# Stick-breaking attention trunk on one core: elementwise work moved from VectorE to GpSimd, and ten instead of nine of sixteen steps with seven products

## The chip, the cores and the metric

The kernel runs on one core of a Trainium2 chip. The core has TensorE (PE, with PEld for the loading of weights), VectorE (DVE), ScalarE (ACT), GpSimd (POOL) and SyncE (SP, which here only issues transfers). The metric is the device time of one execution in microseconds; less is better.

## The reference, cut to what matters

The input `x` has 256 rows of 4096 numbers. One layer of attention is computed and added to it, and a final norm follows (`DEPTH` is 1, so the convolution branch of the file is not reached):

```python
h = x + attn_branch(rms_norm(x, norm_attn), w_in_attn, w_out_attn)
return rms_norm(h, final_norm)

def attn_branch(xn, w_in, w_out):
    q, k, v, g = jnp.split(xn @ w_in, 4, axis=-1)      # 32 heads of 128
    o = stick_breaking_attention(q, k, v)
    return (o * jax.nn.silu(g)) @ w_out

# in the attention, for s < t (strictly causal):
log_fail = where(causal, log_sigmoid(-z), 0)           # z = q k^T / sqrt(128)
a = where(causal, exp(log_sigmoid(z) + suffix_sum(log_fail)), 0);  out = a @ v
```

All of it is float32. The two weight matrices are 4096 x 16384 and 4096 x 4096.

## The kernel before, in words

**Three matmuls for one product.** Every large product is made with float32 values that are split into a high part of type fp32r and a low part, the rest: `h = fp32r(f)`, `l = f - h`. `mm3` (line 780) adds `hh`, `hl` and `lh` in PSUM. ACT makes the high part of a weight block (`wh`, a copy that converts) and DVE the low part (`wl = raw - wh`, by `minus`, line 257). The same is done for the stationary side, the 128 x 128 blocks of x ("forms" `sh`, `sl`) or of the heads (`oh`, `ol`): `both_parts` (line 496).

**Units and steps.** The work of PE is cut into 21 units, each of 16 steps. Units 0 to 15 make the input projection: each has two column blocks of 256 of q and k, and two of gate and v. Then come three units of the output projection with two column blocks of 512 each, and two single ones. A step takes two of the 32 chunks of 128 along the summed dimension. The two row blocks, the two chunks and the two column blocks give a 2 x 2 times 2 x 2 product: a plain step makes eight products, a "mixed" one follows a scheme of Strassen and Winograd. Steps whose number is in `SEVEN` (line 42) need seven products; for them DVE makes sums of weight blocks (`sums`, line 424: three instructions of 128 x 512), and one of the sums comes from an accumulating transfer (`add_block`, line 401: two DMAs issued by POOL that add HBM data to the tile). Other mixed steps take eight products with fewer parts to split: two wide ones (128 x 1024) in place of three wide and one half one (`SEVEN_PARTS`, `EIGHT_PARTS`). Units 0 and 16 are plain, units 1 to 15, 17 and 18 mixed (17 of them), 19 and 20 single, with four products a step.

**Forms.** `blocks_of` (line 528) loads two chunks of x transposed, scales them by the norm's gains, splits them, and calls `sums_of` (line 502) for the sums of blocks that the mixed units need: one instruction of 128 x 256 for an eight-step, four of 128 x 128 for a seven-step, then `both_parts` for what came out. This happens in unit 0. `blocks_of_heads` (line 927) does the same for the output projection with the heads' results, which were spilled to HBM and are fetched again; `again` (line 950) makes one block anew for the single units.

**Heads.** A unit of the input projection yields two heads. `combine` (line 676) adds up the PSUM banks, `gate` (line 763) makes SiLU of the gate, and `head` (line 795) runs one head as a chain: transposes, scores `z`, softplus in four ACT instructions, DVE `f = max(z, 0) + f`, the causal mask of `f` (DVE, minimum with `bound`, a tile of 3e38 and zeros that is made once, line 595), split into `fh` and `fl`, the scan as four matmuls with a triangle of minus ones, two ACT instructions for the weights `a`, the mask of `a` (DVE), and the product with v.

**The end.** `block_out` (line 1007) adds x, sums the squares and multiplies by the gains of the final norm (`h * grow`, DVE); `finish` (line 1107) scales and stores.

**What sets the order.** The program is written out by a planner, `Plan`. Each piece of work is a generator that asks for engine time with a cost and a key; a small event simulation gives each engine the waiting item with the smallest key, and the instructions are issued in that order. `dve`, `act`, `ten` and `moved` (lines 338 to 354) state costs; `until` waits for a name, `take` and `give` are rings of buffers (seven `raw` tiles, five wide and two half pairs of `wh`/`wl`). On the chip each engine runs its own list strictly in that order, with semaphores where data is needed; the planner's times no longer matter there. POOL's list before holds the accumulating DMAs, the spills and fetches of heads, and a few set-up instructions.

In the profile nearly all instructions carry line 115, the line of the planner's helper, so groups are told apart by their tiles.

## Time and profile before

| | |
|---|---|
| median of 3 runs | 1757.85 us (1756.26 to 1759.46) |
| profiled execution, its span from first to last instruction | 1754.0 us |
| what lies around the span (median less span; no other time of the profiled execution is given) | 3.85 us |
| mean granted TensorE clock | 0.997 |
| DMA | 405.86 MB, mean 231 GB/s |

How to read the profile: busy time is the union of an engine's instructions. A group's row gives engine, operation, tiles (written<-read, buffer numbers left out), shapes, count, then busy time and mean ns of one, then the idle time of the engine just before these instructions and what ended it. In the list of waits, "A <- B: total, times, longest" is the time that A's instructions waited for B's. The chain that ended last goes back from the last instruction to what released it, step by step. A row of the timeline is start, duration, engine, instruction. DVE instructions overlap a little when they follow each other, so a group's busy time can be less than count times mean.

### The profile page before, as it was taken

Reading aid. Unit: us, or ns where it says so; the run is one execution under the profiler, and the core shown is the slowest. Engines: PE = TensorE matmul, PEld = TensorE weight load, DVE = VectorE, ACT = ScalarE, POOL = GpSimd, SP = SyncE. Lnnn points to the kernel's source line nnn. Section 1 sums busy time; section 2 is a strip of 40 time slices with the busy share of each in tenths; the row PEclk is TensorE's granted clock in tenths of the full one; section 3 lists DMA queues with packets and bytes.
Section 4 is the critical chain, followed back from the end, with each engine's and each line's share of the span. In section 5 each row is a group of like instructions: output and inputs, shape, how many; then the busy total and the mean of one; then the engine's idle time right before and its main releaser. Section 6 shows DMA issues by size and latency. Waiting matters only on the chain.

```text
span 1754.0 us, 24699 instructions
## 1 busy us (share of the span) xinstructions
PE 1736.9 (99%) x7806; PEld 1427.1 (81%) x7806; DVE 1560.4 (89%) x1971; ACT 1166.4 (67%) x1594; POOL 295.7 (17%) x364
## 2 busy tenths in 40 slices
PE   8999999999999999999999999999999999999997
PEld 6888888888888888888888888888888888888885
DVE  7889999999999999999999999999999997899963
ACT  7975767676767676767676767676767675666543
POOL 0012121111111121211111111111112111111100
PEclk9999999999999999999999999999999999999998
DMA  9968777777777878787878787878786877889874
GB/s 340 316 192 224 230 218 229 223 223 226 222 228 217 239 210 239 208 245 210 240 208 245 208 239 206 242 202 245 200 246 200 262 244 239 229 245 271 257 236 156
DMA packets 242867, 405.86 MB, mean 231 GB/s; under 512 B 27520, under 2 KB 67968, under 8 KB 242736
## 3 DMA queue, kind: packets, MB, share of 16 engines
q1 hardware_dynamic: 193968, 352.15, 60.8%
q0 software_dynamic: 47184, 49.76, 17.3%
q10 hardware_dynamic: 1584, 2.38, 0.4%
q8 instruction: 61, 1.00, 0.2%
q14 instruction: 70, 0.57, 0.1%
HBM read 396.05 MB, written 8.13 MB: 230 GB/s over the span
## 4 chain that ended last, share of the span: by engine, by line
PE 92%; DVE 3%; issue 2%; DMA 2%; ACT 1%; SPq 0%; ACTq 0%; DVEq 0%
PE acc L115 87%; PE z L115 2%; DVE wl L115 2%; PE o L115 2%; DMA raw<-in_w_in_dram 1%; PE tr L115 1%; ACT wh L115 1%; DVE raw L115 0%; ACT h L115 0%; SPq L115 0%; DMA xres<-in_x_dram 0%; DMA raw<-in_w_out_dram 0%; ACTq L115 0%; DVE gv_sb L115 0%; DVE h L115 0%
## 5 line engine op out<-in xcount | busy, mean ns | idle before, releaser
L115 ACT CAST wh<-raw 128x1024 fp32r<-128x1024 f32 (+1 forms) x948 | 886.1, 976 | 476.1 <-issue 173.3
L115 DVE TENSOR_TENSOR wl<-raw,wh 128x1024 fp32r<-128x1024 f32 (+1 forms) x948 | 1032.1, 1131 | 125.3 <-ACT wh L115 118.6
L115 PE MATMUL acc<-wh,sh 128*128 128x512 f32 x1913 | 762.6, 399 | 2.4 <-DVE sh L115 2.1
L115 PE MATMUL acc<-wh,sl 128*128 128x512 f32 x1913 | 746.2, 390 | 0.0
L115 PE MATMUL acc<-wl,sh 128*128 128x512 f32 x1913 | 744.9, 389 | 0.8 <-DVE wl L115 0.8
L115 PEld LDWEIGHTS acc<-wh,sh 128*128 128x128 f32 x1913 | 359.4, 188 | 77.3 <-DVE gv_sb L115 3.9
L115 PEld LDWEIGHTS acc<-wh,sl 128*128 128x128 f32 x1913 | 359.1, 188 | 76.9 <-DVE sl L115 0.8
L115 PEld LDWEIGHTS acc<-wl,sh 128*128 128x128 f32 x1913 | 359.7, 188 | 71.5 <-DVE wl L115 1.5
L115 POOL DMA_DIRECT2D raw<-in_w_in_dram x270 | 236.1, 987 | 1075.7 <-DMA raw<-in_w_in_dram 403.1
L115 DVE TENSOR_TENSOR raw<-raw,raw 128x512 f32<-128x512 f32 x306 | 210.3, 687 | 5.1
L115 PE MATMUL acc<-wh,oh 128*128 128x512 f32 x494 | 193.2, 391 | 0.0
L115 PE MATMUL acc<-wl,oh 128*128 128x512 f32 x494 | 192.4, 389 | 0.6 <-DVE wl L115 0.6
L115 PE MATMUL acc<-wh,ol 128*128 128x512 f32 x494 | 192.3, 389 | 0.0
L115 PEld LDWEIGHTS acc<-wl,oh 128*128 128x128 f32 x494 | 92.8, 188 | 20.5 <-DVE wl L115 1.2
L115 PEld LDWEIGHTS acc<-wh,oh 128*128 128x128 f32 x494 | 92.8, 188 | 19.3 <-DVE gv_sb L115 0.4
L115 PEld LDWEIGHTS acc<-wh,ol 128*128 128x128 f32 x494 | 92.7, 188 | 19.2
L115 DVE TENSOR_TENSOR raw<-raw 128x512 f32<-128x512 f32 x153 | 104.5, 683 | 0.0
L115 POOL DMA_DIRECT2D raw<-in_w_out_dram x36 | 31.6, 992 | 132.5 <-DMA raw<-in_w_out_dram 66.2
L115 ACT ACTIVATE f<-f 128x384 f32<-128x384 f32 x96 | 50.5, 526 | 3.0
L115 DVE SCALAR_TENSOR_TENSOR f<-z,f 128x384 f32<-128x384 f32 x32 | 17.8, 557 | 31.2 <-ACT f L115 31.2
L115 POOL DMA_DIRECT2D p<-spill x33 | 20.3, 696 | 129.6 <-DVE ol L115 94.0
L115 ACT ACTIVATE gl<-gl 128x512 f32<-128x512 f32 x48 | 30.0, 625 | 7.3 <-DVE gl L115 7.3
(90 smaller groups left out, 745.9 us busy)
## 6 DMA issues: line engine op xcount, KB each, us to landing
raw<-in_w_in_dram SPq DMA_DIRECT2D x1020, 256.0 KB, 4.6
raw<-in_w_out_dram SPq DMA_DIRECT2D x256, 256.0 KB, 3.9
raw<-in_w_in_dram POOLq DMA_DIRECT2D x270, 128.0 KB, 5.2
raw<-in_w_out_dram POOLq DMA_DIRECT2D x36, 128.0 KB, 5.6
xr<-in_x_dram SPq DMA_DIRECT2D x16, 256.0 KB, 5.2
xres<-in_x_dram SPq DMA_DIRECT2D x16, 256.0 KB, 5.6
xs<-in_xT_dram SPq DMA_DIRECT2D x15, 256.0 KB, 5.3
spill<-gated POOLq DMA_DIRECT2D x15, 256.0 KB, 3.9
```

What stands on the lines that cost most here:

```text
L115: return self.tc.keep_in_program_order(getattr(self.engine, name)(*args, **kw))
```

## The change

Three things are done at once. `SEVEN` has ten steps and other ones. A cost function for POOL is added to the planner, and these pieces go from DVE to POOL: the subtraction that makes low parts of forms and of `f`, the sums of row blocks and of heads' blocks, the last product of the gate, and the final norm's gains; the two causal masks become an `affine_select` on POOL, and `bound` goes. Some keys are 1 to 3 us earlier. The low parts of weights (`wl`), the sums of weight blocks and all that reads PSUM stay on DVE. Here is the diff:

```diff
--- before.py
+++ after.py
@@ -39,7 +39,7 @@
 
 
 
-SEVEN = (1,3,5,7,8,10,11,13,14)
+SEVEN = (1, 2, 4, 5, 7, 8, 10, 11, 13, 14)
 RAW_BUFS = 7
 PAIRS = 5
 SINGLES = 2
@@ -87,6 +87,10 @@
 
 def scalar_ns(n):
     return 98 + n / 1.2
+
+
+def pool_ns(n):
+    return 200 + 2.2 * n
 
 
 def tensor_ns(n):
@@ -254,8 +258,8 @@
 
     tc.nc.scalar.preload_act_table_set("natural_log_exp_and_others")
 
-    def minus(out_, full, part):
-        nc.vector.tensor_tensor(out=out_, in0=full, in1=part.bitcast(F32), op=ALU.subtract)
+    def minus(out_, full, part, engine=None):
+        (engine or nc.vector).tensor_tensor(out=out_, in0=full, in1=part.bitcast(F32), op=ALU.subtract)
 
 
     units = []
@@ -345,6 +349,11 @@
         cost = sum(scalar_ns(m) for m in n) + 100 * (len(n) - 1)
         return nc.work("scalar", cost, emit, soon() if key is None else key, **kw)
 
+    def pool(emit, n, key=None, **kw):
+        n = n if isinstance(n, tuple) else (n,)
+        cost = sum(pool_ns(m) for m in n)
+        return nc.work("gpsimd", cost, emit, soon() if key is None else key, **kw)
+
 
     FULL_P, FULL_S = (P,) * 2, (W,) * 2
 
@@ -496,15 +505,15 @@
     def both_parts(i, to, f, key):
         h, l = (t[:, to, :] for t in forms[i])
         n = (to.stop - to.start) * P
-        yield act(lambda: nc.scalar.copy(h, f), n, key - 1e3)
-        yield dve(lambda: minus(l, f, h), n, key)
+        yield act(lambda: nc.scalar.copy(h, f), n, key - 3e3)
+        yield pool(lambda: minus(l, f, h, nc.gpsimd), n, key - 2e3)
 
     def sums_of(i, y, what, key):
 
-        tt = nc.vector.tensor_tensor
+        tt = nc.gpsimd.tensor_tensor
         if i not in SEVEN:
             y4 = y.rearrange("p (a b) c -> p a b c", a=KT)
-            yield dve(
+            yield pool(
                 lambda: tt(out=y4[:, :, 0, :], in0=y4[:, :, 0, :], in1=y4[:, :, 1, :], op=ALU.subtract), 2 * P, key
             )
             yield from both_parts(i, slice(4, 6), y4[:, :, 0, :], key)
@@ -516,7 +525,7 @@
                 tt(out=y[:, 3, :], in0=y[:, 0, :], in1=y[:, 3, :], op=ALU.subtract)
                 tt(out=y[:, 2, :], in0=y[:, 2, :], in1=y[:, 3, :], op=ALU.add)
 
-            yield dve(four, (P, P, P, P), key)
+            yield pool(four, (P, P, P, P), key)
             yield from both_parts(i, slice(4, 7), y[:, 1:4, :], key)
             if what == "p":
                 return
@@ -543,7 +552,7 @@
                 nc.scalar.copy(h[:, 0:4, :], y4)
 
             yield act(scaled, (S, S, 2 * S), key - 2e3)
-            yield dve(lambda: minus(l[:, 0:4, :], y4, h[:, 0:4, :]), 2 * S, key)
+            yield pool(lambda: minus(l[:, 0:4, :], y4, h[:, 0:4, :], nc.gpsimd), 2 * S, key - 2e3)
         else:
             for k in range(KT):
                 yield moved("scalar", lambda: nc.scalar.dma_start(y[:, k, :], xT[i][:, k, :]), [S], key - 1,
@@ -591,13 +600,6 @@
 
     ident = ap.tile([P, P], F32, name="ident")
     make_identity(tc.nc, ident)
-
-    bound = ap.tile([P, 1, P], F32, name="bound")
-    nc.gpsimd.memset(bound, 3e38)
-    nc.gpsimd.affine_select(
-        out=bound, in_=bound, compare_op=ALU.is_gt, fill=0.0, base=0,
-        pattern=[[0, 1], [1, P]], channel_multiplier=-1,
-    )
 
     tri_f = ap.tile([P, P], F32, tag="qkl", name="tri_f")
     nc.gpsimd.memset(tri_f, -1.0)
@@ -773,7 +775,7 @@
             lambda: nc.vector.scalar_tensor_tensor(out=l, in0=g, scalar=0.0, in1=l, op0=ALU.min, op1=ALU.subtract), n
         )
         yield act(lambda: nc.scalar.activation(l, l, AF.Exp), n)
-        yield dve(lambda: nc.vector.tensor_tensor(out=g, in0=g, in1=l, op=ALU.mult), n)
+        yield pool(lambda: nc.gpsimd.tensor_tensor(out=g, in0=g, in1=l, op=ALU.mult), n)
         nc.give("qkl")
         nc.tell(("gate", u))
 
@@ -787,10 +789,14 @@
 
 
     BW = 3 * P
-    masked = bound.broadcast_to([P, 2, P])
-
-    def diagonal(f):
-        return f[:, 0 : 2 * P].rearrange("p (a b) -> p a b", a=2)
+    def strict(f):
+
+        d = f[:, 0 : 2 * P].rearrange("p (a b) -> p a b", a=2)
+        return pool(
+            lambda: nc.gpsimd.affine_select(
+                out=d, in_=d, compare_op=ALU.is_gt, fill=0.0, base=0, pattern=[[0, 2], [1, P]], channel_multiplier=-1,
+            ), P,
+        )
 
     def head(u, i):
         yield nc.take("att", "qkh")
@@ -832,12 +838,12 @@
         yield dve(
             lambda: nc.vector.scalar_tensor_tensor(out=f, in0=z, scalar=0.0, in1=f, op0=ALU.max, op1=ALU.add), BW
         )
-        yield dve(lambda: nc.vector.tensor_tensor(out=diagonal(f), in0=diagonal(f), in1=masked, op=ALU.min), 2 * P)
+        yield strict(f)
         yield nc.take("qkh", "qkl")
         fh = ap.tile([P, BW], F32R, tag="qkh", name=f"fh{u}_{i}")
         fl = ap.tile([P, BW], F32R, tag="qkl", name=f"fl{u}_{i}")
         yield act(lambda: nc.scalar.copy(fh, f), BW)
-        yield dve(lambda: minus(fl, f, fh), BW)
+        yield pool(lambda: minus(fl, f, fh, nc.gpsimd), BW)
         nc.give("f")
 
         def scan():
@@ -860,7 +866,7 @@
         yield act(weights_of, (BW, BW))
         nc.give("att")
         nc.start(gated_with(u, i))
-        yield dve(lambda: nc.vector.tensor_tensor(out=diagonal(a), in0=diagonal(a), in1=masked, op=ALU.min), 2 * P)
+        yield strict(a)
         yield nc.until(("gated", u, i))
         o = st["both", u, i][:, 1, :]
         v = lambda t: st["gv", u][:, t, CW + i * P : CW + (i + 1) * P]
@@ -942,7 +948,7 @@
             key = min(place_at(OUT0, s + 1), place_of[OUT0 + 1, s] - 3e3)
             yield nc.until(("used", OUT0, s))
             y = yield from heads_of(s, key, slice(0, 2))
-            yield dve(lambda: nc.vector.tensor_tensor(out=y[:, 0, :], in0=y[:, 1, :], in1=y[:, 0, :], op=ALU.subtract), P, key)
+            yield pool(lambda: nc.gpsimd.tensor_tensor(out=y[:, 0, :], in0=y[:, 1, :], in1=y[:, 0, :], op=ALU.subtract), P, key)
             yield from both_parts(s, slice(1, 2), y[:, 0:1, :], key)
             nc.give("gh")
             nc.tell(("form", "p", s))
@@ -1030,7 +1036,7 @@
         nc.give("att")
         if c < NJ - 1:
             yield nc.until(("grow", c))
-            yield dve(lambda: nc.vector.tensor_tensor(out=h, in0=h, in1=grow[c], op=ALU.mult), W)
+            yield pool(lambda: nc.gpsimd.tensor_tensor(out=h, in0=h, in1=grow[c], op=ALU.mult), W)
         nc.tell(("h", c, t))
 
     def blocks_out(u, c):
```

## The prediction

> **What bounds the kernel now.** I read the page's top first, then the chain of work that ended last, in order of time.
>
> ```profile
> span 1754.0 us, 24699 instructions
> PE 1736.9 (99%) x7806; PEld 1427.1 (81%) x7806; DVE 1560.4 (89%) x1971; ACT 1166.4 (67%) x1594; POOL 295.7 (17%) x364
> PE 92%; DVE 3%; issue 2%; DMA 2%; ACT 1%; SPq 0%; ACTq 0%; DVEq 0%
> ```
> ```profile
> 307.06 51.03 PE acc L115 x225
> ```
>
> PE is busy 99% of the span, and the chain is PE for 92% of it. The piece at 307 us is 225 accumulating matmuls without a gap: 51.03 / 225 = 0.227 us for one, so a product (`mm3`, three matmuls) costs 0.680 us. But DVE is second, at 89%, so I looked at stretches: one unit of the input projection, then the first unit, then the change from the input to the output projection.
>
> ```profile
> 271.60:358.50 86.90, 86.89 (x395) 71.44 (x394) 79.86 (x97) 58.63 (x77) 16.28 (x19) 1.00 0.78 225
> 14.70:101.00 86.30, 86.30 (x382) 70.96 (x383) 71.35 (x122) 74.99 (x141) 3.70 (x4) 1.00 0.91 310
> 1374.00:1527.00 153.00, 152.98 (x687) 126.33 (x686) 133.23 (x204) 100.86 (x146) 22.53 (x35) 1.00 0.79 242
> ```
>
> The columns are the stretch, its length, then the busy time of PE, PEld, DVE, ACT and POOL, the granted clock, the DMA share and GB/s. In a steady unit PE has no gap and DVE has 79.9 of 86.9 us, an idle rest of 7.0 us. ACT has 28 us free, POOL 70, the clock is 1.00 throughout. So PE bounds, and DVE stands 8% behind it.
>
> **The change, part by part.** *Fewer products.* A step in `SEVEN` takes seven products in place of eight. One more of 16 steps is in it, and 17 units are mixed (15 of the input projection, two of the output), so 17 products go.
>
> ```profile
> L115 PE MATMUL acc<-wh,sh 128*128 128x512 f32 x1913 | 762.6, 399 | 2.4 <-DVE sh L115 2.1
> L115 PE MATMUL acc<-wh,oh 128*128 128x512 f32 x494 | 193.2, 391 | 0.0
> ```
>
> The counts agree with the code: 1913 + 494 = 2407 products, 17 x 119 for the mixed units, 2 x 128 for the plain and 2 x 64 for the single ones. They become 2390. **PE loses 17 x 0.680 = 11.6 us**; a steady unit would go from 86.9 to 86.2 us.
>
> *What the tenth step adds on DVE, and what DVE gives away.* These are DVE's groups in the steady unit:
>
> ```profile
> L115 DVE TENSOR_TENSOR wl<-raw,wh 128x1024 fp32r<-128x1024 f32 x41 | 48.3, 1219 | 4.5 <-ACT wh L115 4.5
> L115 DVE TENSOR_TENSOR raw<-raw,raw 128x512 f32<-128x512 f32 x19 | 13.0, 686 | 0.3
> L115 DVE TENSOR_TENSOR raw<-raw 128x512 f32<-128x512 f32 x9 | 6.1, 683 | 0.0
> L115 DVE TENSOR_TENSOR wl<-raw,wh 128x512 fp32r<-128x512 f32 x9 | 6.1, 683 | 0.0
> L115 DVE SCALAR_TENSOR_TENSOR f<-z,f 128x384 f32<-128x384 f32 x2 | 1.1, 558 | 2.1 <-ACT f L115 2.1
> L115 DVE TENSOR_TENSOR fl<-f,fh 128x384 fp32r<-128x384 f32 x2 | 1.1, 550 | 0.0
> L115 DVE TENSOR_TENSOR f<-f,bound 128x256 f32<-128x256 f32 x2 | 0.9, 426 | 0.1
> L115 DVE TENSOR_TENSOR a<-a,bound 128x256 f32<-128x256 f32 x2 | 0.8, 418 | 0.0
> L115 DVE TENSOR_TENSOR gv_sb<-gv_sb,gl 128x512 f32<-128x512 f32 x1 | 0.7, 682 | 0.0
> ```
>
> A seven-step has three wide low parts, one half one and three block sums; an eight-step has two wide ones. The difference is one wide (48.3 / 41 = 1.18 us), one half (0.68) and three sums (3 x 0.69): +3.9 us. Away go `fl`, both masks and the gate product: 1.1 + 0.9 + 0.8 + 0.7 = 3.5 us. DVE goes from 79.9 to 80.3 us of 86.2: the tenth step uses up all that was given away. ACT gets 1.5 casts more against its 28 free us: nothing.
>
> *What the same work costs on POOL.* The trace of before has no two-input arithmetic there. Its nearest rows:
>
> ```profile
> L115 POOL TENSOR_SCALAR_AFFINE_SELECT bound<-bound 128x128 f32<-128x128 f32 x1 | 0.3, 292 | 0.1
> L115 POOL DMA_DIRECT2D raw<-in_w_in_dram x270 | 236.1, 987 | 1075.7 <-DMA raw<-in_w_in_dram 403.1 <-DVE raw L115 226.3 <-DVE wl L115 210.2
> q0 software_dynamic: 47184, 49.76, 17.3%
> ```
>
> For 512 elements the lower end is DVE's 0.68 us, the upper one twice the select's time scaled up (292 x 4 x 2 = 2.3 us, for two inputs). I take what the diff's own planner charges, 200 + 2.2 n ns, because it lies between: 1.33 us for 512, 1.04 for 384, 0.76 for 256, 0.48 for 128, and 0.48 for a mask (292 for half its elements). A steady unit then has 2 x 1.04 + 4 x 0.48 + 1.33 = **5.3 us of arithmetic on POOL**. Its 20 accumulating issues at 0.99 us leave room for that. Throughput of POOL itself is no limit there.
>
> *Whether the two engines can work at once.* No row shows it. The lower end is that POOL's arithmetic costs DVE nothing: while POOL only issues DMAs, `fl` on DVE never varied,
>
> ```profile
> L115 DVE TENSOR_TENSOR fl<-f,fh x32: 544/551/553, 108.7 to 1434.9; 128x384 fp32r<-128x384 f32 x32
> ```
>
> but issuing reads no tile. The upper end is that one stands while the other reads. Then DVE's need is 80.3 + 5.3 = 85.6 us of 86.2, and the waits that DVE has in its own order come on top: 2.1 us per unit for ACT's `f` (row above), and up to 4.5 for ACT's `wh`, which are partly the mark of a DVE that ran ahead. With the 2.1 alone the unit lasts **87.7 us**, 0.8 over before; with all, 92.2. The central choice is 87.7: 15 x 0.8 = **+12 us** in units 1 to 15, in place of PE's -10.2. I take this end since 0.6 us of 86 is all the margin it leaves: a POOL instruction only a little slower than its formula uses that too. The Trainium skill, "SBUF — State Buffer", § "SBUF: two separate sides", speaks against the change here: it says that a DVE instruction with two SBUF inputs and a GpSimd instruction that reads SBUF hold a shared port in turn, each for its whole length. By that rule the sum is the +12, without it the -10.2; no run shown so far decides it.
>
> *Sums and low parts of row blocks, unit 0.* DVE's rows there:
>
> ```profile
> L115 DVE TENSOR_TENSOR xs<-xs 128x128 f32<-128x128 f32 x32 | 9.3, 292 | 1.0
> L115 DVE TENSOR_TENSOR sl<-xs,sh 128x512 fp32r<-128x512 f32 x13 | 9.0, 692 | 4.1 <-ACT sh L115 3.8 <-DMA raw<-in_w_in_dram 0.2
> L115 DVE TENSOR_TENSOR sl<-xs,sh 128x384 fp32r<-128x384 f32 x9 | 5.0, 552 | 0.0
> L115 DVE TENSOR_TENSOR sl<-xs,sh 128x256 fp32r<-128x256 f32 x7 | 2.9, 419 | 0.0
> L115 DVE TENSOR_TENSOR sl<-xs,sh 128x128 fp32r<-128x128 f32 x9 | 2.6, 285 | 0.0
> L115 DVE TENSOR_TENSOR xs<-xs 128x256 f32<-128x256 f32 x6 | 2.5, 422 | 0.1
> ```
>
> 31.3 us leave DVE (71.4 to 40.0). POOL gets, with ten sevens, 40 sums of 128, 6 of 256, 15 low parts of 512, 10 of 384, 10 of 128, 6 of 256: 19.3 + 4.6 + 19.9 + 10.4 + 4.8 + 4.6 = 63.6 us. Side by side that is hidden; taken in turn it is 103.6 in 86.3 us, 17 over. Only the 19.9 us of 512 are due in this unit, the rest one unit later, so I charge their share, 31%: **+5.3** (ends 0 and 17). If `sl` comes late, PE's next step waits for it at once.
>
> *Heads, after 1374 us.* The same with the spilled heads:
>
> ```profile
> L115 DVE TENSOR_TENSOR p<-p 128x128 f32<-128x128 f32 x45 | 13.0, 289 | 1.1
> L115 DVE TENSOR_TENSOR ol<-p,oh 128x512 fp32r<-128x512 f32 x15 | 10.3, 685 | 0.0
> L115 DVE TENSOR_TENSOR ol<-p,oh 128x384 fp32r<-128x384 f32 x9 | 5.0, 550 | 0.0
> L115 DVE TENSOR_TENSOR ol<-p,oh 128x128 fp32r<-128x128 f32 x9 | 2.6, 285 | 0.4 <-ACT oh L115 0.4
> L115 DVE TENSOR_TENSOR p<-p 128x256 f32<-128x256 f32 x6 | 2.5, 417 | 0.0
> L115 DVE TENSOR_TENSOR ol<-p,oh 128x256 fp32r<-128x256 f32 x6 | 2.5, 416 | 0.0
> ```
>
> 35.9 us of these and some 6 more (last heads, first gains, the block that is not spilled) leave DVE, 4 come with the tenth step: 133 to 95. POOL gets 50 sums of 128, 6 of 256, 16 low parts of 512, 10 of 384, 10 of 128, 6 of 256 and 8 us of the last heads and gains, together 78. In turn that is 173 in 153 us, 20 over; due at once are the 21 us of 512, 27%: **+5.4** (ends 0 and 20). The two mixed output units give PE's -1.4. The product with the final gains (14 of 1.33 us) lies long before the last stretch: nothing. `bound` and its two instructions at the start were under the first loads: nothing.
>
> *Keys.* The casts and low parts of forms get keys 2 us earlier. That changes the order on ACT, which has 11 us free even in unit 0: nothing; without that room `sh` would be late, and PE's step with it.
>
> *Transfers.* Each new seven-step adds two accumulating DMAs, 34 in all, 4.5 MB; queue 0 took 17.3% of the span for 49.8 MB, so some 27 us over the whole run, a DMA share of 0.80 for 0.78. Hidden.
>
> *Waits in POOL's order.* POOL works strictly in turn. Behind a mask that waits for DVE's `f` stand the next accumulating DMAs, and the block sums, hence PE, wait for those; behind an accumulate that waits for its load stands a mask or `fl`, and PE's scan waits for that. How tight the scan is, in two heads:
>
> ```profile
> 200.00 0.55 DVE L115 TENSOR_TENSOR fl<-f,fh 128x384 fp32r<-128x384 f32 x1
> 200.89 0.34 PE L115 MATMUL z<-fl,neg_tri 128*128 128x384 f32 x1
> 632.36 0.54 DVE L115 TENSOR_TENSOR fl<-f,fh 128x384 fp32r<-128x384 f32 x1
> 633.70 0.34 PE L115 MATMUL z<-fl,neg_tri 128*128 128x384 f32 x1
> ```
>
> `fl` ends 0.34 and 0.80 us before the scan reads it. A `fl` that waits for half of a wide DVE instruction (0.6 us) eats this; so 0 to 0.3 us for each of 32 heads, 0 to 10 us. I take 0: where DVE already sets the unit, PE's wait is the same time.
>
> **Sum** in the profiled execution: 12 - 1.4 + 5.3 + 5.4 = +21.3 on its span of 1754.0. The median of the times shown, 1757.85, is 3.85 above that span; taking the difference over, **1779 us**.
>
> **The rivals.** *The engines do not hinder each other.* Then PE still bounds, DVE at 80.3 of 86.2 us is as near to it as now, and 11.6 us go: 1757.85 - 11.6 = 1746 us. For it: PE's chain has no gap in a unit where DVE is busy for 92%. It holds as long as DVE loses less than 86.2 - 80.3 - 2.1 = 3.8 of the 5.3 us per unit. Chance 0.30.
>
> *They hinder each other in part*, so that gain and loss meet: PE's -11.6 against some 12 us of waits, 1754 to 1761 us. A measurement of this kernel tells nothing within 0.2%, 3.5 us, from no change. Chance 0.07.
>
> *POOL is kept out, and DVE is not held up.* DVE's instructions follow one another in runs, so POOL might get in only between runs, two or three wide instructions (2.4 to 3.5 us) later. DVE then loses nothing, but each `fl` comes that late, and PE stands in 32 scans for 2.0 to 3.1 us: 65 to 100 us, less 11.6: 1811 to 1846 us. Against it: DVE's 7 us of idle per unit let POOL in. Chance 0.12.
>
> *The tenth step doesn't come in time.* One row of the waits:
>
> ```profile
> POOL raw L115 <- DMA raw<-in_w_in_dram: 403.1, 66, 10.4
> ```
>
> For 403.1 of 1754 us, 23%, an accumulate stands at the head of POOL until its load lands. If the arithmetic, 5.3 us per unit, falls into such stretches and shifts the accumulates and block sums by as much, 23% of it reaches PE: 15 x 1.2 - 11.6 = +7, 1765 us. Against it: accumulates go ahead of other work by their key, 20 us before their step's place. Chance 0.11.
>
> **How the numbers follow.** The forecast, 1779 us, is DVE and POOL taking turns: 0.40. Faster 0.30, within 0.2% 0.07, slower 0.40 + 0.12 + 0.11 = 0.63. The range runs from just under the first rival, 1744, to where the third begins, 1812: the ends of the unknown terms (0 and 17, 0 and 20, the unit's 86.2 to 92.2) reach beyond it only together. The slower cases' own range is 1762 to 1812.
>
> **What would show it.** Right: DVE's two-input rows get longer than 1220 and 685 ns on average, or gaps open before them with POOL as their neighbour; POOL's two-input rows are longer than the formula; PE's busy share falls below 99% and its waits name `wl`, `fl` or `sl`; the steady unit lasts near 87.7 us. Wrong: DVE's means are unchanged and the unit lasts 86.2 us. A unit of 86.9 with waits for block sums alone would speak for the fourth rival, long waits for `fl` for the third. The product count, 2390, tests the first step.

## The result, and the profile after

The median after is **1924.6 us** (1915.31 to 1928.54, four runs), before in the same runs 1757.05 us (1755.36 to 1759.46): ratio **1.0945** [1.0916, 1.0973], 168 us slower. The forecast was 1779 us, its range 1744 to 1812. The direction was right, the size was an eighth of what came. First the top of the page after, with the shares of the chain that ended last:

```profile
span 1922.1 us, 24922 instructions
PE 1778.1 (93%) x7755; PEld 1440.3 (75%) x7755; DVE 1559.6 (81%) x1745; ACT 1187.6 (62%) x1631; POOL 734.2 (38%) x719
...
PE 7%; DVE 3%; issue 2%; ACT 1%; DMA 1%; ACTq 0%; SPq 0%; DVEq 0%
```

PE is no longer at 99%. No other engine has taken its place: DVE fell from 89% to 81%, ACT from 67% to 62%. So time went into waits. POOL is "busy" for 439 us more, where 719 - 364 = 355 instructions came. The chain that ended last can be followed for only some 14% of the span, so I didn't build on it. The stretches tell more; the columns are those of the prediction (stretch, length, busy PE, PEld, DVE, ACT, POOL, clock, DMA, GB/s):

```profile
404.88:500.29 95.41, 88.62 (x391) 72.30 (x390) 81.32 (x95) 59.87 (x80) 31.04 (x28) 0.96 0.72 207
1073.63:1163.92 90.29, 87.22 (x391) 70.64 (x390) 84.11 (x95) 60.09 (x80) 24.90 (x29) 1.00 0.76 219
...
14.70:117.00 102.30, 92.61 (x392) 71.75 (x393) 56.19 (x50) 75.32 (x141) 87.78 (x87) 1.00 0.82 268
```

A steady unit lasts 95.4 us where it was 86.9. PE is idle in it for 6.8 us, and its granted clock is 0.96 on the mean. The second row is the one unit of this kind that lasts 90.3. The third is unit 0: POOL busy for 86% of it, DVE for 55%. The 168 us divide up at the gate's DVE instruction (`gl<-gv_sb,gl`), of which each unit has one: up to the first of them 118.3 us where it was 102.6 (**+16**); from there to the last 1431.5 where it was 1308.0 (**+124**, 15 units); after it 372.3 where it was 343.4 (**+29**).

Is DVE held up by POOL, as the forecast had it? DVE's groups by shape:

```profile
L119 DVE TENSOR_TENSOR wl<-raw,wh 128x1024 fp32r<-128x1024 f32 x808 | 984.4, 1265 | 291.7 <-ACT wh L119 280.4 <-DMA raw<-in_w_in_dram 8.1 <-DMA xres<-in_x_dram 1.5
L119 DVE TENSOR_TENSOR raw<-raw,raw 128x512 f32<-128x512 f32 x340 | 235.8, 694 | 4.3
```

Hardly: over the whole run the wide low parts take 1265 ns for 1220 and the sums 694 for 687, and in the steady unit above the wide ones take what they took before:

```profile
L119 DVE TENSOR_TENSOR wl<-raw,wh 128x1024 fp32r<-128x1024 f32 x43 | 50.3, 1219 | 12.2 <-ACT wh L119 12.2
```

But over the run DVE now waits 280 us for ACT's casts. It is POOL that was held up. All 16 of its gate products, in one row (min/median/max of the duration in ns):

```profile
L119 POOL TENSOR_TENSOR gv_sb<-gv_sb,gl x16: 1292/8051/8057, 120.7 to 1553.8; 128x512 f32<-128x512 f32 x16
```

The same instruction takes 1.29 us once and 8.05 in most units; a wait for a port counts as busy here. In the unit that begins at 500.29 us the timeline shows what is beside it and what follows (a selection of the rows; start, duration, engine, instruction, then the idle time before it and its releaser):

```profile
497.85 0.68 DVE L119 TENSOR_TENSOR raw<-raw 128x512 f32<-128x512 f32 x1
498.45 6.37 DVE L119 TENSOR_TENSOR wl<-raw,wh 128x1024 fp32r<-128x1024 f32 x6
500.29 8.06 POOL L119 TENSOR_TENSOR gv_sb<-gv_sb,gl 128x512 f32<-128x512 f32 x1 [6.50 <-ACT gl L119]
504.73 0.69 DVE L119 TENSOR_TENSOR raw<-raw,raw 128x512 f32<-128x512 f32 x1
504.85 0.33 PE L119 MATMUL z<-fh,neg_tri 128*128 128x384 f32 x1
505.33 0.69 DVE L119 TENSOR_TENSOR wl<-raw,wh 128x512 fp32r<-128x512 f32 x1
505.94 0.68 DVE L119 TENSOR_TENSOR raw<-raw,raw 128x512 f32<-128x512 f32 x1
506.54 0.69 DVE L119 TENSOR_TENSOR raw<-raw 128x512 f32<-128x512 f32 x1
508.30 1.78 POOL L119 DMA_DIRECT2D raw<-in_w_in_dram  x2
509.44 1.66 POOL L119 TENSOR_TENSOR fl<-f,fh 128x384 fp32r<-128x384 f32 x1
511.16 0.69 PE L119 MATMUL z<-fl,neg_tri 128*128 128x384 f32 x1 [5.98 <-POOL fl L119]
512.26 0.49 ACT L119 ACTIVATE a<-z 128x384 f32<-128x384 f32 x1 [9.23 <-PE z L119]
512.49 0.63 PE L119 MATMUL acc<-wl,sh 128*128 128x512 f32 x1
512.92 0.63 PE L119 MATMUL acc<-wh,sl 128*128 128x512 f32 x1
...
514.27 2.36 DVE L119 TENSOR_TENSOR wl<-raw,wh 128x1024 fp32r<-128x1024 f32 x2 [7.05 <-ACT wh L119]
515.42 0.40 PE L119 MATMUL acc<-wh,sl 128*128 128x512 f32 x1
515.65 0.38 PE L119 MATMUL o<-ident,gv_sb 128*128 128x128 f32 x2
```

DVE runs these eleven instructions with two SBUF inputs without a gap, the last ending at 506.54 + 0.69 = 507.23 us. The product came at 500.29 and ends 1.1 us after that run, about as long as it takes alone. Behind it in POOL's list stand two accumulating DMAs and the first head's `fl`. PE has done the scan's `fh` half and stands for 5.98 us; with it stand the next casts on ACT (behind `a<-z`, 9.23) and DVE (7.05). Then comes a second loss: PE's matmuls start 0.43 us apart instead of 0.227 until 515.4. The waits, summed:

```profile
DVE wl L119 <- ACT wh L119: 286.6, 224, 7.1
...
ACT a L119 <- PE z L119: 152.6, 29, 9.2
...
PE z L119 <- POOL fl L119: 90.0, 30, 6.0
```

So PE stood 90.0 us in 30 waits for `fl`, 6 us in the first head of 13 units.

### The profile page after: what moved, and what is told of

Read it like the earlier page. It is cut to its first block, busy times and chain, and to the rows that moved or that the text cites. A ratio compares the mean times of both kernels' runs of the same rounds, so it can differ in the third digit from the quotient of the medians.

```text
span 1922.1 us, 24922 instructions
## 1 busy us (share of the span) xinstructions
PE 1778.1 (93%) x7755; PEld 1440.3 (75%) x7755; DVE 1559.6 (81%) x1745; ACT 1187.6 (62%) x1631; POOL 734.2 (38%) x719
## 5 line engine op out<-in xcount | busy, mean ns | idle before, releaser
L119 DVE TENSOR_TENSOR wl<-raw,wh 128x1024 fp32r<-128x1024 f32 (+1 forms) x982 | 1109.2, 1177 | 297.9 <-ACT wh L119 286.6
L119 ACT CAST wh<-raw 128x1024 fp32r<-128x1024 f32 (+1 forms) x982 | 904.5, 971 | 380.0 <-issue 188.5
L119 POOL DMA_DIRECT2D raw<-in_w_in_dram x300 | 263.6, 991 | 623.8 <-DMA raw<-in_w_in_dram 250.8
L119 PEld LDWEIGHTS acc<-wh,sl 128*128 128x128 f32 x1898 | 361.7, 191 | 86.8 <-POOL sl L119 10.3
L119 DVE TENSOR_TENSOR raw<-raw,raw 128x512 f32<-128x512 f32 x340 | 235.8, 694 | 4.3
L119 POOL TENSOR_TENSOR gv_sb<-gv_sb,gl 128x512 f32<-128x512 f32 x16 | 109.9, 6870 | 89.8 <-ACT gl L119 89.7
L119 DVE TENSOR_TENSOR raw<-raw 128x512 f32<-128x512 f32 x170 | 120.0, 706 | 0.0
L119 PEld LDWEIGHTS acc<-wl,oh 128*128 128x128 f32 x492 | 93.7, 190 | 32.8 <-DVE wl L119 13.7
L119 ACT ACTIVATE a<-z 128x384 f32<-128x384 f32 x32 | 15.7, 491 | 152.6 <-PE z L119 152.6
L119 PE MATMUL z<-fl,neg_tri 128*128 128x384 f32 x64 | 25.1, 441 | 90.0 <-POOL fl L119 90.0
L119 PEld LDWEIGHTS z<-fl,neg_tri 128*128 128x128 f32 x64 | 15.4, 240 | 101.1 <-POOL fl L119 101.1
L119 POOL TENSOR_TENSOR ol<-p,oh 128x128 fp32r<-128x128 f32 (+3 forms) x50 | 58.1, 1200 | 50.7 <-ACT oh L119 36.3
```

What stands on the lines that cost most here:

```text
L119: return self.tc.keep_in_program_order(getattr(self.engine, name)(*args, **kw))
```

## The experiments

Two theories come first in the expectations. **A**: a POOL instruction that reads SBUF can be shut out for a whole gapless run of DVE instructions with two SBUF inputs, and the scan, hence PE, stands for `fl`. **B**: the tenth step and the fuller instruction lists make the units long, and POOL's long rows only mark it. (A third, **C** in two of the texts: the product is slow by itself, because of its operands.) Times of before beside these runs were 1755.6 to 1757.1 us. Diffs are against the kernel after.

### One part undone at a time

```diff
-        yield pool(lambda: nc.gpsimd.tensor_tensor(out=g, in0=g, in1=l, op=ALU.mult), n)
+        yield dve(lambda: nc.vector.tensor_tensor(out=g, in0=g, in1=l, op=ALU.mult), n)
```

> The changed kernel with the gate's last product back on DVE, all else as changed. Theory A (POOL can't start reading while DVE's two-input instructions follow each other without a gap; the gate's product sits out such a run for 8 us, and fl stands behind it in POOL's list): the 6.0 us that PE waits for fl in the first head of 13 units go, with the lower clock behind them (2.4 us more PE time per unit); the one unit whose product was short came 5.1 us sooner than the others, so 13 x 5.1 to 13 x 8.4 us are gained: 1816 to 1858 us. Theory B (the forecast's: the two take turns, DVE has too much to do): DVE gets 0.6 us per unit and loses a 1.3 us hindrance, at most 15 x 1.3 = 20 us gained: 1905 us or more.

1897.23 us, 1.0802 [1.0787, 1.0817]: between the two bands. The lockout had only moved to the next POOL instruction, `fl` itself:

```profile
L119 POOL TENSOR_TENSOR fl<-f,fh x32: 1005/1832/6405, 123.8 to 1570.8; 128x384 fp32r<-128x384 f32 x32
```

In the first heads it takes 5.6 or 6.4 us, and PE waits 56 us for it. The gate's product isn't the cause by itself; whatever POOL instruction arrives during the run can be hit.

```diff
-        yield pool(lambda: minus(fl, f, fh, nc.gpsimd), BW)
+        yield dve(lambda: minus(fl, f, fh), BW)
```

> The changed kernel with the low part fl of both heads back on DVE; the gate's product stays on POOL. Theory A: fl needs the buffer that the gate's product reads, so DVE stops at fl until POOL is through; that gap lets POOL in, the product takes 2 to 4 us in place of 8, and PE's wait for fl falls from 6 to some 1 to 2 us: 1830 to 1870 us. Theory B: DVE has 1.1 us more to do per unit and is hindered 2 us less: 1905 us or more. Theory C (the product takes 8 us by itself, because of its operands): it still takes 8 us, now with DVE standing at fl as well: no faster than 1915 us.

1818.12 us, 1.0348 [1.0332, 1.0364]: `fl` off POOL gives back 106 us, a little more than A said. The gate's product is still hindered, but for 5.07 us and not 8.05, for DVE's own list now holds an instruction that waits for it (`fl` on DVE needs the buffer that the gate gives back; DVE waits 16.5 us in 14 units), so the run is cut there.

```diff
-            yield pool(four, (P, P, P, P), key)
+            yield dve(four, (P, P, P, P), key)
...
-        tt = nc.gpsimd.tensor_tensor
+        tt = nc.vector.tensor_tensor
...
-        yield pool(lambda: minus(l, f, h, nc.gpsimd), n, key - 2e3)
+        yield dve(lambda: minus(l, f, h), n, key)
```

> The changed kernel with the sums and low parts of row blocks and of heads' blocks back on DVE, with their old keys; heads, gate and final gains stay on POOL. Measured from the traces, the changed kernel is 16 us later than before at the first gate (unit 0) and loses 29 us after the last one. If POOL's forms are the cause of these, 16 and some 20 to 25 of the 29 us come back: 1880 to 1890 us. If DVE's lack of time was the cause (theory B), moving 75 us of work back to it gains nothing: 1915 us or more.

1892.52 us, 1.0773 [1.0759, 1.0788], just above the band: the forms of unit 0 and of the heads cost 32 us. The gate's product stays at 8.05 us, so this part is separate.

### One part alone

Ten steps, with nothing moved to POOL:

```diff
-SEVEN = (1,3,5,7,8,10,11,13,14)
+SEVEN = (1, 2, 4, 5, 7, 8, 10, 11, 13, 14)
```

(against the kernel before)

> The kernel before with the ten new steps in SEVEN and nothing moved to POOL. By the forecast's terms PE loses 11.6 us and DVE needs 79.9 + 3.9 = 83.8 of 86.2 us per unit, 85.9 with its 2.1 us of waits for f: 1746 us if DVE keeps up. If the tenth step is itself too much for DVE, as the change's offloading supposes, a unit takes up to 83.8 + 2.1 + 4.5 = 90.4 us: up to 1810 us.

1758.48 us, 1.0012 [1.0004, 1.0021]. PE has 17 products less to do, 11.6 us by the count, and nothing is gained. A steady unit of this run, from gate to gate, and the waits of PE's weight loads:

```profile
368.53:455.17 86.64, 86.16 (x392) 70.96 (x391) 82.69 (x103) 59.86 (x79) 18.04 (x21) 1.00 0.80 228
```
```profile
PEld acc L119 <- DVE wl L119: 27.0, 36, 1.6
```

DVE is busy for 82.7 of 86.64 us, and PE stands for the 0.5 us that it has less to do: two units of before, 173.68 us from 280.88 to 454.56, come to 86.84 each. Over the whole run the weight loads wait 27.0 us for low parts, where before they waited 2.8 us, 4 times. From the first gate to the last the run gains 3.4 us; it loses 1.5 before that and 4.4 after. B's first half falls: the tenth step alone costs 0.1%.

Ten steps and the two masks alone on POOL; all else is undone, such as

```diff
-        yield pool(lambda: minus(fl, f, fh, nc.gpsimd), BW)
+        yield dve(lambda: minus(fl, f, fh), BW)
...
-            yield pool(four, (P, P, P, P), key)
+            yield dve(four, (P, P, P, P), key)
```

> Ten steps, and only the two masks of each head on POOL, all else on DVE. The masks took 0.41 us alone and 0.7 to 2.1 us beside DVE's runs in the runs so far; the mask of f has some microseconds to spare in the first head, the mask of a about 1 us. Theory A: PE waits 0 to 1 us per head, 0 to 32 us, less 1.7 us of DVE time per unit, so 1745 to 1785 us. If masks were as harmful as the other moves (a reading select is kept out like a product of two inputs), over 1800 us.

1762.11 us, 1.0037 [1.0023, 1.0052], 3.6 us more than ten steps alone. The mask of `f` takes 0.40 us in the median, the mask of `a` between 0.40 and 2.66.

Gate, `fl` and masks back on DVE; forms and gains stay on POOL, with ten steps:

```diff
-        yield pool(lambda: nc.gpsimd.tensor_tensor(out=g, in0=g, in1=l, op=ALU.mult), n)
+        yield dve(lambda: nc.vector.tensor_tensor(out=g, in0=g, in1=l, op=ALU.mult), n)
...
+        return dve(lambda: nc.vector.tensor_tensor(out=d, in0=d, in1=masked, op=ALU.min), 2 * P)
...
-        yield pool(lambda: minus(fl, f, fh, nc.gpsimd), BW)
+        yield dve(lambda: minus(fl, f, fh), BW)
```

> The changed kernel with the whole head and the gate back on DVE (masks, fl, gate's product); sums and low parts of blocks and the final gains stay on POOL. Theory A: in units 1 to 15 nothing of POOL's arithmetic is left, so they run as in the kernel with ten steps alone (1758 us), and only unit 0 and the output part lose, 16 and 20 to 29 us as the traces showed: 1790 to 1805 us. Theory B, by which DVE lacks time in the units: 3.5 us per unit more on DVE, 1790 us plus up to 50.

1796.83 us, 1.0234 [1.0218, 1.0249], in A's band. Against ten steps alone, forms and gains cost 38 us; the heads' part of the change costs the other 1924.6 - 1796.8 = **128 us**. The trace puts them in their places: without the heads' part the steady units last 86.6 to 87.0 us again and the stretch from the first gate to the last 1306.5. The first gate comes at 117.8 us, against 104.1 with ten steps alone, and what follows the last one lasts 371.8 us, against 347.8. So most of the +16 and the +29 of the division above are forms and gains, which weren't tried apart, and the +124 is the heads' part.

```diff
-SEVEN = (1, 2, 4, 5, 7, 8, 10, 11, 13, 14)
+SEVEN = (1, 3, 5, 7, 8, 10, 11, 13, 14)
```

> The changed kernel with all that moved still on POOL, but with the nine steps of before in SEVEN. Ten steps alone on DVE made 1.8 us more than before, so if the moves cause the loss by themselves, some 165 us over before stay: 1900 to 1930 us (theory A, POOL waits out DVE's runs, which are nearly as long with nine steps). If it is the tenth step together with the moves that fills DVE (theory B), nine steps bring most of the loss back: under 1830 us.

1819.03 us, 1.0362 [1.0346, 1.0377], all moves with the old nine steps. By the time alone A is beaten here. The trace says why:

```profile
L119 POOL TENSOR_TENSOR gv_sb<-gv_sb,gl x16: 1527/1537/1984, 122.5 to 1454.8; 128x512 f32<-128x512 f32 x16
```

With this choice of steps the gate's product takes some 1.5 us in every unit. So the mechanism can be hit or missed by what DVE happens to run, and my wording of A, that any run shuts POOL out, was too strong.

The same with the forms back on DVE (the diff of the run with forms back, above), heads, gate and gains on POOL:

```diff
-SEVEN = (1, 2, 4, 5, 7, 8, 10, 11, 13, 14)
+SEVEN = (1, 3, 5, 7, 8, 10, 11, 13, 14)
...
-        yield pool(lambda: minus(l, f, h, nc.gpsimd), n, key - 2e3)
+        yield dve(lambda: minus(l, f, h), n, key)
```

> Nine steps as before, heads, gate and final gains on POOL, sums and low parts of forms back on DVE. With ten steps the forms cost 32 and 38 us. If they cost the same with nine, 1819 - 35 = 1784 us, and the heads alone account for some 27 us where their products are not kept out; if forms cost less with nine, 1800 us or more.

1788.26 us, 1.0181 [1.0164, 1.0198]. So with nine steps the forms cost 31 us and the rest 32, even without a lockout of 8 us: a steady unit lasts 88.4 us (373.70 to 462.11), 1.5 over before.

### Is it the run? A measurement by itself

These small kernels compute nothing of the reference. A stage of the first: DVE writes `g` and then runs `k` instructions; POOL multiplies `g`, and the next stage needs the product.

```python
def stage(n, vector, k, gpsimd):
    ...
    nc.vector.tensor_tensor(out=g, in0=go, in1=b[:, 0:512], op=ALU.add)
    for i in range(k):
        vector(n, i)
    go = gpsimd(n, g)
```

> A kernel that computes nothing of the reference: one POOL instruction, released together with a run of k DVE instructions, in thirteen stages one after the other. Stages 1 and 2: product of 128x512 on POOL with DVE idle. 3 to 7: beside runs of 1, 2, 4, 8, 16 subtractions of 128x1024 with both inputs in SBUF. 8: beside 16 of 128x512 with one input in PSUM. 9: beside 16 scalings of 128x1024 with one input. 10: beside 8 subtractions with one instruction that reads PSUM after each second one. 11 to 13: a select of one input alone, beside 8 subtractions, beside 16 that read PSUM. Theory A: alone 1.2 to 1.3 us; beside a run it ends about 1.2 us after the run's end, so k x 1.14 + 1.2 us: 2.3, 3.5, 5.8, 10.3 and 19.4 us; beside PSUM readers 1.3 us as alone. Theory B (turns, one each): never over 1.2 + 1.3 = 2.5 us, and DVE's own instructions get longer. Theory C (the operands make the product slow): alone as long as beside a run.

POOL's rows in order of time; beside them DVE ran 0, 8 and 16 two-input subtractions of 128 x 1024, then 16 that read PSUM and SBUF, then 16 scalings with one input, and at last 8 subtractions with an instruction that reads PSUM behind every second one:

```profile
9.86 1.26 POOL L19 TENSOR_TENSOR pr<-go,b 128x512 f32<-128x512 f32 x1 [0.81 <-DVE go L19]
...
25.05 2.18 POOL L19 TENSOR_TENSOR pr<-go,b 128x512 f32<-128x512 f32 x1 [4.03 <-DVE go L19]
35.80 19.21 POOL L19 TENSOR_TENSOR pr<-go,b 128x512 f32<-128x512 f32 x1 [8.57 <-DVE go L19]
55.81 1.27 POOL L19 TENSOR_TENSOR pr<-go,b 128x512 f32<-128x512 f32 x1 [0.81 <-DVE go L19]
65.98 1.65 POOL L19 TENSOR_TENSOR pr<-go,b 128x512 f32<-128x512 f32 x1 [8.90 <-DVE go L19]
77.28 3.32 POOL L19 TENSOR_TENSOR pr<-go,b 128x512 f32<-128x512 f32 x1 [9.66 <-DVE go L19]
```

In that last stage DVE's list begins like this:

```profile
77.13 2.35 DVE L19 TENSOR_TENSOR gap<-a,b 128x1024 f32<-128x1024 f32 x2
79.40 0.68 DVE L19 TENSOR_TENSOR psout<-ps,b 128x512 f32<-128x512 f32 x1
```

Alone the product takes 1.26 us, which rules out C, and beside 16 two-input instructions **19.21**; that run, of 18.24 us or 16 times 1.14, isn't slowed. Beside PSUM readers it takes 1.27. In the last stage it is kept out of both subtractions and ends at 80.60, 1.2 us after the PSUM reader began and about as long as it takes alone: such a reader lets it in. So the lockout is real, and two-input instructions in SBUF do it. Whether one-input ones can is open: 1.65 us is a wait of 0.4, and one contest that POOL won would look the same. A select on POOL, with its one input, fares alike: 0.63 us alone, 1.56 beside 8 subtractions, 0.63 beside PSUM readers. The Trainium skill, "SBUF — State Buffer", § "SBUF: two separate sides", says that such a DVE instruction and a GpSimd instruction that reads SBUF exclude each other, and that whichever starts first has the port for its whole length. The trace agrees with the exclusion (1.26, 1.27, 19.21 us). If whoever waits came next, the wait would end with one DVE instruction, 1.2 us here; the sentence doesn't say who comes next, and in the measurement POOL can lose every handover of a run. But it can also win: beside runs of 1, 2, 4 and 8 it took 2.17 or 2.18 us, and then DVE stands: the run of 8 took 10.22 us, 1.1 more than 8 times 1.14.

### What decides whether POOL is let in?

```python
    if columns:
        nc.gpsimd.memset(junk[:, 0:columns], 0.0)
    ...
    nc.gpsimd.tensor_tensor(out=go, in0=g, in1=b[:, 0:512], op=ALU.mult)
...
for n in range(1, 9):
    stage(n, 0, (8, 16)[n % 2])
for n in range(16):
    stage(9 + n, 64 + 80 * n, 8)
```

> A second kernel that computes nothing of the reference. Stages 1 to 8: the same POOL product beside runs of 16 and 8 subtractions in turn, four times each. Stages 9 to 24: beside runs of 8, with a POOL write of 64, 144, ... 1264 columns ahead of the product, so that it arrives at another point of DVE's current instruction each time (some 70 ns further each stage, over a whole period of 1.14 us). If the length of the run decides: all runs of 16 keep POOL out (19 us), all of 8 let it in after one instruction (at most 2.4 us). If the point of arrival decides: stages of both lengths come out both ways, and in 9 to 24 the product either takes up to 2.4 us or sits out the whole rest of the run (8 to 9 us), with little between.

Stages with runs of 16 and 8 in turn, and then 16 stages with a POOL write ahead of the product, which waits for a one-column write on DVE ahead of the run. The runs of 16 now let it in (2.17 us, four times) and the runs of 8 shut it out (10.13, four times): the length of the run isn't it. With the writes all 16 products were let in (1.26 to 2.30 us); from this I took the idea that a POOL write ahead protects.

```diff
...
+            nc.gpsimd.memset(tick[:, 0:1], 0.0)
+            nc.gpsimd.tensor_tensor(out=g, in0=g, in1=l, op=ALU.mult)
...
```

> The changed kernel, nothing moved back and nothing added on DVE; POOL writes one number per row directly ahead of the gate's product, of each fl and of each mask of a, and waits for ACT at that write (ACT gives it a mark by a copy of one column). If a read that follows another POOL instruction is always let in after one DVE instruction, as in 16 stages of 16, the gate's product takes at most 2.4 us in all units, the 6 us waits for fl go, and the time falls to 1810 to 1865 us. If the point of arrival alone decides, the product still takes 8 us in most units: 1915 to 1930 us.

The same in the kernel after, with such a write also ahead of `fl` and of the mask of `a`, each released by a one-column copy on ACT: 1930.09 us, 1.0987 [1.097, 1.1003], and the product still takes 7.94 us in most units. So a POOL write ahead doesn't protect there; in the small kernel it may have been DVE's tiny write, which wasn't tried apart.

```python
    for i in range(k):
        ...
        nc.vector.tensor_tensor(out=w, in0=a, in1=b, op=ALU.subtract)
    ...
    nc.scalar.copy(t, g)
    nc.scalar.copy(junk[:, 0:columns], x2[:, 0:columns])
    nc.scalar.copy(u, a[:, 0:512])
    ...
    nc.gpsimd.tensor_tensor(out=go, in0=t, in1=u, op=ALU.mult)
...
for n in range(1, 41):
    stage(n, 32 * n, 10)
```

> A third kernel that computes nothing of the reference: 40 stages, in each a POOL product beside a run of 10 subtractions of 128x1024 with both inputs in SBUF. The product is released by ACT, 27 ns later from stage to stage, so its arrival goes over almost a whole DVE instruction (1.14 us). If the point of arrival decides, some stages let it in after the current DVE instruction (1.3 to 2.4 us) and some keep it out to the end of the run, in connected ranges of arrival. If being a fresh arrival is enough, most are kept out; if ACT's release makes no difference to a DVE one, about half are.

Forty equal stages of ten DVE instructions, in which ACT releases POOL 27 ns later each time relative to the run:

```profile
206.08 10.71 POOL L19 TENSOR_TENSOR pr<-t,u 128x512 f32<-128x512 f32 x1 [11.40 <-ACT u L19]
219.31 1.60 POOL L19 TENSOR_TENSOR pr<-t,u 128x512 f32<-128x512 f32 x1 [2.52 <-ACT u L19]
232.35 10.65 POOL L19 TENSOR_TENSOR pr<-t,u 128x512 f32<-128x512 f32 x1 [11.45 <-ACT u L19]
245.58 1.54 POOL L19 TENSOR_TENSOR pr<-t,u 128x512 f32<-128x512 f32 x1 [2.58 <-ACT u L19]
```

Strictly in turn, all forty: let in with 1.3 to 2.4 us, shut out with 10.1 to 11.1. The moment of arrival, moved by 1.05 us in all, nearly a whole DVE instruction (1.14), decides nothing.

```python
for k, writes in ((9, 0), (10, 0), (9, 1), (10, 1)):
    for _ in range(10):
        n += 1
        stage(n, 600, k, writes)
```

> Computes nothing of the reference. Four times ten equal stages of a POOL product, released by ACT, beside a run of DVE subtractions: runs of 9 (an even number of DVE instructions per stage), of 10 (odd), of 9 and of 10 with one more POOL instruction in each stage, a write ahead of the stage's wait. If the number of DVE instructions decides, the ten stages with runs of 9 all come out alike and those with runs of 10 in turn, whatever POOL does. If POOL's number decides, the first twenty go in turn and the last twenty come out alike. If it is a turn that each contest passes on, all forty go in turn.

Runs of 9 and 10, with and without one POOL write more per stage: again strictly in turn, 1.5 to 2.2 us and 9.5 (runs of 9) or 10.6 (runs of 10). So the count of instructions of either engine isn't it. In equal stages the outcome looks like a state that each contest passes on.

### Does letting POOL in repair the kernel?

```diff
...
+            nc.vector.memset(tick, 0.0)
...
```

(behind every `wl`; `tick` is one column, 982 fills in all)

> The changed kernel, nothing moved back; DVE writes one number per row (a fill of a 128x1 tile) behind each low part of weights, which costs DVE time (981 of them). Theory A, that POOL is kept out while DVE's two-input instructions follow each other directly: each fill is a place to get in, so the gate's product takes 1.3 to 2.5 us in place of 8, the 6 us waits for fl go, and the time falls in spite of the added work, to 1820 to 1870 us. If a fill is too short to let POOL in, or DVE's load is the cause (theory B): 1925 us plus up to 60.

1863.76 us, 1.061 [1.0596, 1.0625]: DVE's busy time rises from 1559.6 to 1601.7 us, and the kernel gets **61 us faster** than after. The gate's product takes 1.68 us. B, by which DVE has too much to do, can't explain that. But the next run has the same effect without a fill inside the run, so it isn't shown that a fill lets POOL in by standing between two instructions.

```diff
...
+            nc.vector.memset(tick, 0.0)
+            nc.vector.scalar_tensor_tensor(out=l, in0=g, scalar=0.0, in1=l, op0=ALU.min, op1=ALU.subtract)
...
```

> The changed kernel with one more DVE instruction per unit, a fill of one column (0.06 us) ahead of the gate's minimum, some 2 us before the gate's product arrives; a unit then has 95 DVE instructions in place of 94. If the number of DVE instructions decides, the gate's product is kept out in every second unit: 8.0 and 1.7 us in turn, and six or seven units win some 5 to 8 us: 1870 to 1895 us. If it does not, the product takes 8 us as before: 1915 to 1930 us.

One fill of 0.06 us per unit, in the gate, ahead of the eleven instructions and not among them: 1856.91 us, 1.0573 [1.0555, 1.0591], 68 us faster than after. I had expected units in turn or no effect; every unit changed:

```profile
L119 POOL TENSOR_TENSOR gv_sb<-gv_sb,gl x16: 1657/1668/2267, 120.8 to 1485.7; 128x512 f32<-128x512 f32 x16
```

A steady unit lasts 90.3 us, as in the one unit of after with a short product. So the lockout of the gate's product is worth some 5 us in each of 13 units, and one tiny instruction turns it off. The list of the run behind it is the same as in after. What changes there is who stands: DVE's six wide low parts, which took 6.37 us while POOL was shut out, take 9.11 with the product and `fl` let in.

```profile
394.00 9.11 DVE L119 TENSOR_TENSOR wl<-raw,wh 128x1024 fp32r<-128x1024 f32 x6
```

So this run is still 60 us above the one with the heads' part undone (1796.83), and a unit 3.7 us above 86.6. PE's waits in such a unit add up to 3.1 us, for `wl`, for the gated heads and for `fl`; which of the remaining moves makes them wasn't tried.

### Could PE's saving be had by relieving DVE elsewhere?

```diff
-        yield act(lambda: nc.scalar.activation(l, g, AF.Abs), n)
-        yield act(lambda: nc.scalar.activation(l, l, AF.Exp, scale=-1.0), n)
+        yield act(lambda: nc.scalar.activation(l, g, AF.Exp, scale=-1.0), n)
...
-        yield dve(
-            lambda: nc.vector.scalar_tensor_tensor(out=l, in0=g, scalar=0.0, in1=l, op0=ALU.min, op1=ALU.subtract), n
-        )
-        yield act(lambda: nc.scalar.activation(l, l, AF.Exp), n)
+        yield act(lambda: nc.scalar.activation(l, l, AF.Exp, scale=-1.0), n)
```

(SiLU's logarithm in another form, so that the gate's minimum leaves DVE; ten steps, and all that went to POOL is back on DVE)

> Ten steps, nothing on POOL, and the gate's minimum and subtraction taken off DVE another way: ACT makes exp(-ln(1 + exp(-g))) in three instructions in place of four around a DVE one. With ten steps alone a unit had 82.9 us of DVE and lasted 86.9, PE's waits for wl among them, with PE's need at 86.2. If DVE sets the unit there, 0.7 us less on DVE is 0.7 us per unit: 15 x 0.7 = 10 us, so 1748 us. If it is the order of bursts and not the sum, nothing changes: 1758 us.

1763.79 us, 1.0042 [1.0029, 1.0054], a miss. A unit, from gate to gate (275.02 to 362.20), lasts 87.2 us, and DVE is busy for 82.5 of it, where ten steps alone had 82.7 of 86.64. (The 82.9 and 86.9 of the expectation are of a fixed stretch of 86.9 us, not of that run's own unit.) So of the 0.7 us that should leave DVE 0.2 did, and the time rose. Whether it is DVE's sum or the moments at which its pieces come that keeps PE's 11.6 us from being had, this run doesn't show; I didn't follow it further.

The same with nine steps:

```diff
-SEVEN = (1, 2, 4, 5, 7, 8, 10, 11, 13, 14)
+SEVEN = (1, 3, 5, 7, 8, 10, 11, 13, 14)
```

> The same gate on ACT with the nine steps of before, as a control: PE sets the unit there without a gap, so 0.7 us less on DVE changes nothing: 1755 to 1758 us.

1756.12 us, 1.0 [0.9991, 1.0009]: no difference, as PE bounds. No version that was run is faster than the kernel before.

## Why the prediction was right and wrong

**What failed** is the step "Whether the two engines can work at once". Its upper end was that one engine "stands while the other reads", one instruction at a time, which gave 87.7 us for a unit. That end isn't the worst: POOL can be shut out for a whole run, 8.05 us for a product that takes 1.26. The victim is then POOL and not DVE, whose wide rows stay at 1219 ns in the steady unit. The unit came to 95.4 us, beyond even the 92.2 with all of DVE's waits. Where POOL is let in, DVE does stand, as the step has it: with one fill per unit its six low parts take 9.11 us for 6.37. With nine steps and the forms back on DVE a unit lasts 88.4 us, near the 87.7; but PE's waits in it, 0.9 us for `a` and 0.3 for the gated heads, don't name DVE's low parts, so that nearness may be luck. The second failure hangs on the first: for PE's wait for `fl` I took "0 to 0.3 us for each of 32 heads", and then 0, since DVE would set the unit anyway. It was 5.98 us in the first head.

**The mechanism stood among the rivals**, as "POOL is kept out, and DVE is not held up", at 1811 to 1846 us and a chance of 0.12; the sign given for it, long waits for `fl`, came. The sentence against it, that "DVE's 7 us of idle per unit let POOL in", is where the chance went wrong: idle time of a unit says nothing of the place. In the quoted unit DVE's idle time, 7.05 us at once, comes after the run and is the effect of the stall. And its price counted only `fl`; the gate's product, ahead of `fl` in POOL's list, was the one caught longest.

**What a steady unit came to.** 95.4 for 86.9 us, +8.5: the product saved, -0.7; PE's waits for `fl`, 6.0 in the first head and 0.25 in the second; some 2 us at half the clock after the stall (4.2 us from 511.2 at a granted 0.51, so 2.1 lost). That makes +7.6; 0.9 I can't place. The half clock was in no term.

**Prices of POOL's instructions** were right for the instruction alone: 1.33 us charged for 512 elements, 1.26 measured. In the kernel they weren't, and where POOL's neighbours on DVE read two SBUF inputs, the wait for them is inside the duration:

```profile
L119 POOL TENSOR_TENSOR fl<-f,fh 128x384 fp32r<-128x384 f32 x32 | 57.6, 1801 | 32.1 <-ACT fh L119 32.1
...
L119 POOL TENSOR_TENSOR xs<-xs 128x128 f32<-128x128 f32 x40 | 30.4, 760 | 2.7
...
L119 POOL TENSOR_TENSOR sl<-xs,sh 128x384 fp32r<-128x384 f32 x10 | 15.0, 1500 | 2.5 <-ACT sh L119 2.5
```

0.76 us for the 0.48 charged, 1.50 for 1.04, 1.80 for 1.04.

**Unit 0 and the heads' blocks** were forecast at +5.3 and +5.4. Undoing them in the changed kernel gave back 32 us, adding them and the gains to ten steps cost 38. By the runs with ten steps alone and with the heads' part undone, +5.3 was +13.7 (104.1 to 117.8 us at the first gate) and +5.4 was +24.0, the gains in it (347.8 to 371.8 after the last one). In unit 0 the mechanism was right, the pieces of a step come late: PE waits 6.0 us for `sl` and its weight loads 10.3, the casts of sums wait 26.0 us for POOL's sums, and POOL is busy for 87.8 of 102.3 us. The size was not: I had charged only 31% of the overlap. Why the heads' blocks cost 24 was not followed.

**PE's -11.6 us** was counted right (2390 products) and could not be had: ten steps alone give 1758.48. The first rival, 1746, rested on the same gain, and the prediction took it for free that DVE delivers low parts in time. With DVE at 82.7 of 86.64 us it didn't, nor at 81.7 of 86.85 with the masks on POOL; whether 80.3, the figure of that rival, would be enough was not shown. **The tenth step not in time** (0.11) isn't what came: its sign was a unit of 86.9 us with waits for block sums alone, and the unit lasts 95.4 with waits for `fl`. But the choice of steps took part: of the two that were tried, only this one lets the gate's product fall into its long wait, 1819 us with nine, 1924.6 with ten.

**The range** was too narrow by the prediction's own terms. It says that their ends reach beyond 1812 us only together; but a unit of 92.2, one of these ends, is 15 x 5.3 = 79.5 us over before and gives some 1837 us alone.

**Right** were: the argument that POOL reading SBUF and DVE with two SBUF inputs hinder each other, and the sign, this in part by luck, since it came by another path: not DVE's own time set the unit, but PE that stood for POOL. Right were also transfers, `bound` and POOL's DMA issues, none of which shows among PE's larger waits.

**What stays open**: what decides a contest. In equal stages POOL is let in and shut out strictly in turn, with runs of 9 or 10, for every moment of arrival that was tried and with one POOL write more; but four wins followed one another in the first small kernel and sixteen in the second, and in the kernel after the same side loses in 13 of 16 units until one fill is added.

## What to carry to other kernels

Before work is moved to GpSimd, look at what VectorE runs without a gap at the moment when the piece arrives: if these are instructions with two SBUF inputs, charge the piece with the whole run as the upper end (here 8 us for 1.3), and follow POOL's list to the first engine that waits for anything behind it. A free engine with 70 us to spare is no cover if the piece lies in a chain that PE waits for. A saving on the bounding engine has to be checked against the second: here VectorE was busy for 82.7 of 86.64 us with ten steps, and a saving of 11.6 us on PE brought nothing.

## What the runs showed of the hardware that was not expected

- A POOL instruction that reads SBUF can lose every handover of a gapless run of two-input DVE instructions: 19.21 us beside 16 of them for 1.26 alone. One that reads PSUM let it in (3.32 us, behind two subtractions). In equal stages the outcome alternates, forty of forty in two kernels; where POOL wins, DVE stands (10.22 us for a run of 8 instead of 9.1).
- A single 0.06-us fill per unit on DVE, some 3 us ahead of the stalled instruction, made the kernel 68 us faster; how it turns the outcome is open.
- After PE had stood for 6 us, its matmuls started 0.43 us apart instead of 0.227 for some 4 us. The Trainium skill, "TensorE: Matmul & The Clock Gate", Part 1, says that the array falls to half its clock after an idle window of about 3.4 us and needs about as long a busy one to come back. The trace agrees: a granted 0.51 from 511.2 to 515.4, and full spacing from 516.1 on.
